# A hybrid RWKV/attention layer on one core: recurrence outputs moved to PSUM tiles of their own, two small copies to ScalarE, and the inverse stage called one wave later

## The chip, the core and the metric

The kernel runs on one core of a Trainium2 chip. The metric is device microseconds of one execution. The core's engines are TensorE (PE, with its weight load shown as PEld), VectorE (DVE), ScalarE (ACT), GpSimd (POOL) and the queue that issues most of the DMAs (SP). Each engine runs its own instructions in the order in which the program lists them, and waits on semaphores for the others.

## What is computed

Two layers of a backbone for 256 context tokens and 1024 latent tokens of width 1024. Each layer projects the stream, runs three kinds of heads (a bidirectional RWKV-7 recurrence, grouped-query attention, neighbourhood attention), gates them, projects back and normalises. What the change touches is the recurrence:

```python
def _rwkv7_step(S, inp):
    r, w, k, v, kk, b = inp
    sa = jnp.einsum('bhvk,bhk->bhv', S, kk)
    S = S * w[:, :, None, :] - sa[..., None] * b[:, :, None, :] + v[..., None] * k[:, :, None, :]
    return S, jnp.einsum('bhvk,bhk->bhv', S, r)
...
    S_f, y_f = lax.scan(_rwkv7_step, S0_f, (r, decay[:, :, 0], kd[:, :, 0], v, kk, bd[:, :, 0]))
    S_b, y_b = lax.scan(_rwkv7_step, S0_b, (r, decay[:, :, 1], kd[:, :, 1], v, kk, bd[:, :, 1]), reverse=True)
    return S_f, S_b, y_f + y_b
```

## The kernel before

The recurrence (`rwkv`, once per layer) is done in blocks. A **step** covers 32 tokens of both directions, a **wave** is four steps (128 tokens), and there are 10 waves per layer. Its parts, with the letters by which the last loop (L790 on) calls them:

- `wave_pre` (p) loads a wave's tensors and makes decays (`lp`, `iv`), the keys `kb`, the matrices `G` and the step decays `dc` (L575). `wave_gram` (g) multiplies `kb` with `G` and masks the result back into `G` (L616). `wave_kt` (k) transposes `kb` and copies it into `S` (L630).
- `wave_low` (l) writes triangular blocks to DRAM (`ls_d`) and reads them back in another layout (`lin`, L601). `wave_inv` (i) copies `lin` to `nn` (L635, L636), inverts in 15 rounds of two DVE operations (L644, L646) and sends the result through DRAM to `di`. `wave_merge` (m) makes `tt` from `di` with two groups of matmuls (`mg`, L675) and DVE operations L678 and L680.
- `wave_chain` is the serial part. Each step: 12 matmuls `rs` (L704), ACT copies them to `rsb` (L710), 12 matmuls `sa` (L715), four copies into the step's state `X` (L721), 12 matmuls `z` (L725), and two DVE operations that make the next step's `X` (L730). The output `y` of a step (`out_step`: 12 matmuls L742 and a copy to `yst`, L744) is put off through the list `pend` until the `rs` matmuls of the next step are written. In layer 1 the first two waves have no output.
- `out_block` adds both directions of `y` for one block of 128 tokens, normalises them, transposes them on PE (`pso`, L780; read by ACT at L782) and writes `yg_d`. Two blocks follow each of waves 6 to 9; in layer 0 two follow wave 1.

`X` has three buffers, so the loads of a step's `X` (four DMAs per step, L697, and four POOL memsets, L699) wait until the step three before is read to the end, by its `y` too. In PSUM the chain has one bank, `ch`: `rs`, `sa`, `z` and `y` are column ranges of it. All other stages take tiles in turn from the pool `pa`, which has **two** buffers (tag `pp`).

The projections that remain and the whole attention are written behind `rwkv`; a list scheduler sets each engine's order when the kernel is built, so the attention's instructions stand between those of the recurrence. Behind the recurrence stands what reuses its memory: the output weights (`wf<-wout`, L1110) and the output projection (L1159 on).

Of the kernel before, what the change touches and what calls it, by code (L numbers as in the profile page):

```python
# [8 lines left out]
F32 = mybir.dt.float32  # L9
# [34 lines left out]
def body(tc, a):  # L44
    nc = tc.nc
# [12 lines left out]
    pp = const.tile([128, DEPTH, NPC], F32, tag="pp", name="pp")  # L58
# [453 lines left out]
    def rwkv(l, lay):  # L512
# [3 lines left out]
        r2 = es.enter_context(tc.tile_pool(name=f"rx{l}", bufs=1, reuse_waits="tile"))  # L516
        r3 = es.enter_context(tc.tile_pool(name=f"ry{l}", bufs=1, reuse_waits="tile"))
        pb = es.enter_context(tc.tile_pool(name=f"pb{l}", bufs=1, space=PSUM))
        pa = es.enter_context(tc.tile_pool(name=f"pa{l}", bufs=2, space=PSUM))
        bank = pb.tile([128, 512], F32, tag="ch", name="ch")  # L520
        rs = sa = bank[:, 0:192].rearrange("p (c v) -> p c v", c=3)
        z = bank[:, 0:384].rearrange("p (d c v) -> p d c v", d=2, c=3)
        y = bank[:, 320:512].rearrange("p (c v) -> p c v", c=3)
        zw = lay["zw"]
        tri = rp.tile([128, 2, 128], F32, tag="tri", name="tri")
        nc.sync.dma_start(out=tri, in_=a["tri"])
# [6 lines left out]
        for g in S:  # L533
            for p in range(2):
                o = slice(64 * p, 64 * p + 64)
# [10 lines left out]
        def wave_pre(w):  # L546
            dc = r2.tile([128, 2, 4, 3], F32, tag="dc", name="dc", bufs=4)
            prep[w] = dict(dc=dc, d=[], g=[])
            for d in range(2):
                t0 = 128 * wave_block(w, d)  # L550
                need_r = not (last and t0 < TC)
                ld = {}
                for nm, ix in (("r", 0), ("kk", 1), ("kd", 2 + d), ("bd", 4 + d)):
                    if nm == "r" and not need_r:
                        continue
                    t = r3.tile([128, 3, 128], F32, tag="ld" + nm, name="ld" + nm, bufs=2 if nm == "r" else 1)
                    nc.sync.dma_start(out=t, in_=rw_d[ix, :, :, t0:t0 + 128].rearrange("c p t -> p c t"))
                    ld[nm] = t
                ps = pa.tile([128, 384], F32, tag="pp", name="psz")
                zs = r2.tile([98, 128], F32R, tag="zs", name="zs")  # L560
                nc.gpsimd.dma_start(out=zs, in_=zs_d[d, :, t0:t0 + 128])
                nc.tensor.matmul(out=ps, lhsT=zs, rhs=zw[d], start=True, stop=True)
                th = r3.tile([128, 384], F32, tag="th", name="th")
                nc.scalar.activation(out=th, in_=ps, func=AF.Tanh, scale=0.5)
                nc.vector.tensor_scalar(out=th, in0=th, scalar1=1.0, scalar2=None, op0=ALU.add)
                cu = pa.tile([128, 3, 4, 32], F32, tag="pp", name="pcu")
                for c in range(3):
                    nc.tensor.matmul(out=cu[:, c], lhsT=th[:, 128 * c:128 * c + 128], rhs=tri[:, d], start=True, stop=True)
                lp = r2.tile([128, 3, 4, 33], F32, tag="lp", name="lp")
                iv = r3.tile([128, 3, 4, 32], F32, tag="iv", name="iv")  # L570
                o = 1 - d
                nc.gpsimd.memset(lp[:, :, :, 32 * d:32 * d + 1], 1.0)
                nc.scalar.activation(out=lp[:, :, :, o:o + 32], in_=cu, func=AF.Exp, scale=-0.5 * EM05)
                nc.scalar.activation(out=iv, in_=cu, func=AF.Exp, scale=0.5 * EM05)
                nc.vector.tensor_copy(dc[:, d], lp[:, :, :, 32 * o:32 * o + 1].rearrange("p c j o -> p (j o) c"))  # L575
                kb = r2.tile([128, 3, 4, 64], F32, tag="kb", name="kb", bufs=2)
                v4 = lambda t: t.rearrange("p c (j t) -> p c j t", t=32)
                nc.vector.tensor_tensor(out=kb[:, :, :, 32 * d:32 * d + 32], in0=v4(ld["kd"]), in1=iv, op=ALU.mult)
                nc.gpsimd.tensor_tensor(out=kb[:, :, :, 32 - 32 * d:64 - 32 * d], in0=v4(ld["bd"]), in1=iv, op=ALU.mult)
                g = G[(2 * w + d) % 6]  # L580
                for p in range(2):
                    rs_ = slice(64 * p, 64 * p + 64)
                    gv = g[rs_, :, :, p, :].rearrange("q j c f -> q c j f")
                    nc.gpsimd.memset(g[64 - 64 * p:128 - 64 * p, :, :, p, 0:64 if need_r else 32], 0.0)
                    nc.gpsimd.tensor_tensor(out=gv[:, :, :, 0:32], in0=v4(ld["kk"])[rs_], in1=lp[rs_, :, :, d:d + 32], op=ALU.mult)
                    if need_r:
                        nc.gpsimd.tensor_tensor(out=gv[:, :, :, 32:64], in0=v4(ld["r"])[rs_], in1=lp[rs_, :, :, o:o + 32], op=ALU.mult)
                prep[w]["g"].append(g)
                prep[w]["d"].append((kb, 64 if need_r else 32))
# [93 lines left out]
        def wave_chain(w):  # L683
# [5 lines left out]
            for j in range(4):  # L689
# [10 lines left out]
                for c in range(3):  # L700
                    for d in range(2):
                        for p in range(2):
                            q = QSA[d][p]
                            nc.tensor.matmul(out=rs[q:q + 32, c, :], lhsT=gs[d][:, jc[d], c, p, 0:32], rhs=x[:, d, c, p, :],  # L704
                                             start=True, stop=True, tile_position=(0, q))
                for f in pend:
                    f()
                pend.clear()
                rsb = r2.tile([128, 3, 64], F32, tag="rsb", name="rsb")
                nc.scalar.copy(rsb, rs)  # L710
                for c in range(3):
                    for d in range(2):
                        for p in range(2):
# [21 lines left out]
            pend.clear()  # L735

        def out_step(w, j, x, jc, gs, yst):
            for c in range(3):
                for d in range(2):
                    for p in range(2):  # L740
                        q = QSA[d][p]
                        nc.tensor.matmul(out=y[q:q + 32, c, :], lhsT=gs[d][:, jc[d], c, p, 32:64], rhs=x[:, d, c, p, :],  # L742
                                         start=True, stop=True, tile_position=(0, q))
            nc.vector.tensor_copy(yst[:, j], y)  # L744
            if j == 3:
                for d in range(2):
                    for p in range(2):
                        q = QSA[d][p]
                        nc.sync.dma_start(out=y_d[d, 128 * w:128 * w + 128, :][:, 192 * p:192 * p + 192].rearrange("(j t) f -> t j f", t=32),
                                          in_=yst[q:q + 32].rearrange("t j c v -> t j (c v)"))  # L750
# [39 lines left out]
        for w in range(-3, NW):  # L790
            if w >= 0:
                wave_chain(w)
            for c in "kpglmi":
                v = w + (2 if c in "km" else 3)
                if 0 <= v < NW:
                    stages[c](v)
            for i, b in enumerate((11 - w, w) if w > 5 else (0, 1) if w == 1 and not last else ()):
                out_block(b, i)
# [593 lines left out]
```

## Time and profile before

| | us |
|---|---|
| runs of before | 2510.26 (median), 2495.68, 2519.41 |
| the profiled execution | 2503.84, its span 2502.0 |
| recurrence of layer 0, first `rs` to last `y` | about 402 to 1085 |
| recurrence of layer 1, the same | about 1673 to 2336 |
| busy share of PE, DVE, POOL, ACT | 88%, 66%, 47%, 39% |

The span is that of one profiled execution. A row of a view names an engine, a line of the kernel and the tile written and read; "idle before" is time that the engine stood still, and the arrow names what ended it. A matmul of 32-bit data is counted as two instructions, so 12 matmuls show as x24. PEclk is the granted share of TensorE's full clock.

### The profile page before, as it was taken

The numbers are of one execution on the slowest core, as the hardware profiler recorded it, in microseconds if no ns is written. First come the engines' busy times: TensorE is split into PE (matmuls) and PEld (weight loads), VectorE is DVE, ScalarE is ACT, GpSimd is POOL, SyncE is SP. The second block draws the span as 40 slices with busy tenths as digits, with TensorE's granted clock in tenths as the row PEclk, the third lists the DMA queues.
The fourth block names the chain that finished last, engine by engine and source line by source line (L and its number), as shares of the span: only waits on it lengthen the run. The fifth ranks groups of instructions, "written<-read, shape, count | busy, mean of one in ns | idle before, by whom it ended". The sixth has DMA issues, their size and how long they took to land.

```text
span 2502.0 us, 57786 instructions
## 1 busy us (share of the span) xinstructions
PE 2204.5 (88%) x22616; PEld 1655.1 (66%) x22616; DVE 1660.7 (66%) x3183; ACT 978.7 (39%) x2074; POOL 1188.3 (47%) x1438
## 2 busy tenths in 40 slices
PE   6989999986878798999899999999868788989897
PEld 4777898764555555555797777787655555645497
DVE  5686524546887778676386795524478787777746
ACT  3333413333544344554234434223334434445522
POOL 3464426335564454453246356334456545545443
PEclk9999999997898899989999999999869989989899
DMA  7345335446555434452332455335555444432332
GB/s 278 111 158 167 109 92 127 114 108 142 120 123 115 109 93 106 125 156 60 99 100 90 138 166 184 104 88 130 143 113 126 92 105 107 96 81 66 122 113 93
DMA packets 448241, 298.17 MB, mean 119 GB/s; under 512 B 249600, under 2 KB 395880, under 8 KB 446944
## 3 DMA queue, kind: packets, MB, share of 16 engines
q1 hardware_dynamic: 439936, 281.71, 41.2%
q0 software_dynamic: 7392, 10.28, 1.5%
q8 instruction: 178, 2.92, 0.5%
q10 hardware_dynamic: 640, 2.49, 0.4%
q14 instruction: 95, 0.78, 0.1%
HBM read 198.37 MB, written 91.79 MB: 116 GB/s over the span
## 4 chain that ended last, share of the span: by engine, by line
PE 47%; DVE 21%; DMA 14%; issue 6%; ACT 5%; SPq 4%; POOL 3%; DVEq 0%; POOLq 0%; ACTq 0%
PE pj L203 5%; PE pj L204 5%; PE pj L205 5%; PE y L921 4%; DMA ls_d<-G 3%; PE sm L867 2%; PE st L936 2%; DVE mx L869 2%; DVE e L646 2%; DMA lin<-ls_d 2%; PE pj L1159 2%; PE st L937 2%; DVE G L616 2%; PE pj L1161 2%; PE pj L1160 2%
## 5 line engine op out<-in xcount | busy, mean ns | idle before, releaser
L204 PE MATMUL pj<-hlo,wh 128*128 128x512 f32 (+1 forms) x1072 | 403.0, 376 | 12.3 <-DVE hlo L480 7.2
L203 PE MATMUL pj<-hhi,wh 128*128 128x512 f32 (+1 forms) x1072 | 404.9, 380 | 7.4 <-ACT qr L348 4.7
L205 PE MATMUL pj<-hhi,wl 128*128 128x512 f32 (+1 forms) x1072 | 400.8, 375 | 0.0
L204 PEld LDWEIGHTS pj<-hlo,wh 128*128 128x128 f32 x1072 | 205.6, 192 | 54.9 <-DVE hlo L480 7.3
L169 POOL TENSOR_TENSOR wl<-wf,wh 128x512 fp32r<-128x512 f32 x104 | 142.2, 1371 | 209.3 <-ACT wh L168 194.6
L203 PEld LDWEIGHTS pj<-hhi,wh 128*128 128x128 f32 x1072 | 205.0, 192 | 52.8 <-issue 7.0
L943 ACT ACTIVATE pt<-st 128x512 f32<-128x512 f32 (+1 forms) x292 | 165.2, 582 | 174.7 <-PE st L937 171.4
L205 PEld LDWEIGHTS pj<-hhi,wl 128*128 128x128 f32 x1072 | 205.5, 192 | 37.7 <-issue 3.1
L869 DVE TENSOR_REDUCE mx<-sm 128x1 f32<-128x512 f32 (+1 forms) x372 | 198.9, 553 | 39.2 <-PE sm L867 37.5
L921 PE MATMUL y<-pt,v 128*64 128x256 f32 (+1 forms) x1392 | 221.2, 406 | 2.7 <-ACT pt L943 2.3
L936 PE MATMUL st<-q,k 128*128 128x512 f32 (+3 forms) x376 | 168.0, 451 | 22.6 <-DVE am L110 6.5
L867 PE MATMUL sm<-k,q 128*128 128x256 f32 (+2 forms) x436 | 169.7, 432 | 19.5 <-DVE mx L869 7.8
L1159 PE MATMUL pj<-yh,wh 128*128 128x256 f32 x576 | 160.0, 294 | 11.8 <-ACT yh L1133 10.7
L1160 PE MATMUL pj<-yl,wh 128*128 128x256 f32 x576 | 164.7, 289 | 0.8 <-POOL yl L1134 0.8
L1161 PE MATMUL pj<-yh,wl 128*128 128x256 f32 x576 | 163.2, 288 | 0.0
L921 PEld LDWEIGHTS y<-pt,v 128*64 128x64 f32 x1392 | 97.1, 146 | 96.3 <-issue 66.3
L950 POOL TENSOR_TENSOR acc<-acc,pt 128x512 f32<-128x512 f32 x80 | 104.5, 1306 | 116.5 <-ACT pt L943 109.9
L937 PE MATMUL st<-q,k 65*128 65x512 f32 (+3 forms) x376 | 151.3, 406 | 1.4 <-ACT q L881 1.3
L867 PEld LDWEIGHTS sm<-k,q 128*128 128x128 f32 x436 | 84.8, 210 | 81.6 <-issue 21.0
L616 DVE TENSOR_TENSOR G<-gt,msk 64x192 f32<-64x192 f32 (+1 forms) x320 | 110.5, 345 | 39.6 <-PE gt L611 28.7
L699 POOL MEMSET X<- 32x192 f32 x320 | 82.9, 259 | 93.2 <-PE ch L742 68.8
L630 ACT COPY S<-kt 64x192 f32<-64x192 f32 x320 | 100.4, 314 | 55.4 <-PE ch L725 28.7
(276 smaller groups left out, 5137.2 us busy)
## 6 DMA issues: line engine op xcount, KB each, us to landing
wf<-win SPq DMA_DIRECT2D x104, 256.0 KB
wm<-wmod SPq DMA_DIRECT2D x32, 512.0 KB
yf<-yg_d SPq DMA_DIRECT2D x72, 128.0 KB
wt<-wm SPq DMA_DIRECT2D x8, 1024.0 KB
gate_d<-o SPq DMA_DIRECT2D x32, 256.0 KB
wf<-wout SPq DMA_DIRECT2D x16, 512.0 KB
ldkk<-rw_d SPq DMA_DIRECT2D x40, 192.0 KB
ldkd<-rw_d SPq DMA_DIRECT2D x40, 192.0 KB
```

Of the source, the lines that this page charges most:

```text
L203: nc.tensor.matmul(out=ps[:, :n], lhsT=wh, rhs=hhi[:, k, t0:t0 + n], start=(k == 0), stop=False)
L204: nc.tensor.matmul(out=ps[:, :n], lhsT=wh, rhs=hlo[:, k, t0:t0 + n], start=False, stop=False)
L205: nc.tensor.matmul(out=ps[:, :n], lhsT=wl, rhs=hhi[:, k, t0:t0 + n], start=False, stop=(k == KT - 1))
L867: nc.tensor.matmul(out=sp_[:, :o], lhsT=q[0][:, qc:qc + 128], rhs=k[0][:, c0:c0 + o], start=True, stop=True)
L869: nc.vector.tensor_reduce(out=mx[:, n_:n_ + 1], in_=sp_[:, :o], op=ALU.max, axis=AX.X)
L921: mm = nc.tensor.matmul(out=y[64 * i:64 * i + 64, a0:a1], lhsT=v[:, t, :], rhs=pt[:, p0:p0 + a1 - a0], start=start, stop=stop and at == le ...
L936: nc.tensor.matmul(out=o, lhsT=k[0][:, 128 * t:128 * t + 128], rhs=q[0][:, qa:qb], start=True, stop=False)
L937: mm = nc.tensor.matmul(out=o, lhsT=k[1][0:65, 128 * t:128 * t + 128], rhs=q[1][0:65, qa:qb], start=False, stop=True)
L943: nc.scalar.activation(out=pt[:, :w], in_=sp_[:, :w], func=AF.Exp)
L1159: nc.tensor.matmul(out=p_, lhsT=wh[m][:, k], rhs=yh, start=(x_ == 0), stop=False)
L1160: nc.tensor.matmul(out=p_, lhsT=wh[m][:, k], rhs=yl, start=False, stop=False)
L1161: nc.tensor.matmul(out=p_, lhsT=wl[m][:, k], rhs=yh, start=False, stop=(x_ == KT - 1))
```

## The change

Three edits. The recurrence output gets a tile `py` of the pool `pa` instead of columns of `ch`, its copy to `yst` goes from DVE to ACT, and the put-off outputs are written behind the copy of `rs` instead of ahead of it. The copy of the step decays `dc` goes from DVE to ACT. The stages of a loop pass are called in another order: `i` comes first, for wave w + 2, where it came last, for wave w + 3.

```diff
-        y = bank[:, 320:512].rearrange("p (c v) -> p c v", c=3)
...
-                nc.vector.tensor_copy(dc[:, d], lp[:, :, :, 32 * o:32 * o + 1].rearrange("p c j o -> p (j o) c"))
+                nc.scalar.copy(dc[:, d], lp[:, :, :, 32 * o:32 * o + 1].rearrange("p c j o -> p (j o) c"))
...
+                rsb = r2.tile([128, 3, 64], F32, tag="rsb", name="rsb")
+                nc.scalar.copy(rsb, rs)
                 for f in pend:
                     f()
                 pend.clear()
-                rsb = r2.tile([128, 3, 64], F32, tag="rsb", name="rsb")
-                nc.scalar.copy(rsb, rs)
...
         def out_step(w, j, x, jc, gs, yst):
+            y = pa.tile([128, 3, 64], F32, tag="pp", name="py")
...
-            nc.vector.tensor_copy(yst[:, j], y)
+            nc.scalar.copy(yst[:, j], y)
...
-            for c in "kpglmi":
-                v = w + (2 if c in "km" else 3)
+            for c in "ikpglm":
+                v = w + (2 if c in "ikm" else 3)
```

First place: PE in the last wave of layer 1, from the middle of the wave to its last step. `X_17548` (after: `X_17588`) is the state buffer of the wave's first and last step, `X_17549` and `X_17550` (after: `X_17589`, `X_17590`) those of the two between. Before:

```order
L704 MATMUL ch<-X_17550,G_17530 32x64 x2
L704 MATMUL ch<-X_17550,G_17531 32x64 x2
...
L742 MATMUL ch<-X_17549,G_17530 32x64 x2
L742 MATMUL ch<-X_17549,G_17531 32x64 x2
...
L715 MATMUL ch<-rsb,tt 32x64 x12
...
L725 MATMUL ch<-X_17550,S_17538 64x64 x6
...
L704 MATMUL ch<-X_17548,G_17530 32x64 x2
```

After:

```order
L780 MATMUL pso<-c_ident,yo 128x128 x3
L742 MATMUL py<-X_17588,G_17570 32x64 x2
...
L867 MATMUL sm<-k_25912,q_26520 128x512
L867 MATMUL sm<-k_25912,q_26520 128x256
L921 MATMUL y<-pt_26767,v 64x256
...
L969 MATMUL ls<-acc_26529,onec 32x256 x2
...
L742 MATMUL py<-X_17589,G_17570 32x64 x2
...
L703 MATMUL ch<-X_17588,G_17570 32x64 x2
L742 MATMUL py<-X_17590,G_17570 32x64 x2
```

Before, each step's `y` stood directly behind the next step's `rs`. After, the `y` of the wave's first three steps stand together behind the second `pso` of the blocks that follow the wave before, and the last step's `rs` stands among them; where no block follows a wave, they stand behind the second `mg` group of the wave after.

Second place: DVE in layer 1, from the masks of the last wave (`G<-gt,msk`) to its inverse (`nn<-lin`, then `tmp<-nn,e`). Before:

```order
L616 TENSOR_TENSOR G_17531<-gt,msk 64x3x64 x4
L950 TENSOR_TENSOR acc_25860<-acc_25860,pt_25956 128x512
L770 TENSOR_SCALAR sm<-sm 128x6
L869 TENSOR_REDUCE mx<-sm 128x1
L771 TENSOR_TENSOR yo<-yo,sm 128x384
...
L636 COPY nn<-lin 64x256
L869 TENSOR_REDUCE mx<-sm 128x1
L644 TENSOR_TENSOR tmp<-nn,e 128x15
```

After:

```order
L615 TENSOR_TENSOR G_17571<-gt,msk 64x3x64 x4
L869 TENSOR_REDUCE mx<-sm 128x1 x2
L950 TENSOR_TENSOR acc_25599<-acc_25599,pt_25866 128x512
L776 TENSOR_TENSOR yo<-yo,sm 128x2x3x64
...
L635 COPY nn<-lin 64x256
L869 TENSOR_REDUCE mx<-sm 128x1
L643 TENSOR_TENSOR tmp<-nn,e 128x15
```

Between the last masks and the second `nn` stand eleven rows before and six after, and the same kinds of rows; in none of the 20 waves does the `nn` of a wave move behind another wave's masks.

## Rows read from the trace of the kernel before

**Rows 1.** The page's first part: busy us (share of the span) and instructions.

```profile
PE 2204.5 (88%) x22616; PEld 1655.1 (66%) x22616; DVE 1660.7 (66%) x3183; ACT 978.7 (39%) x2074; POOL 1188.3 (47%) x1438
```

**Rows 2.** Busy time by stretch: both recurrences, and layer 1's passage to the output.

```profile
core 0: us, PE busy (x) PEld busy (x) DVE busy (x) ACT busy (x) POOL busy (x), PEclk, DMA share, GB/s
400.00:1100.00 700.00, 594.09 (x8668) 414.07 (x8668) 490.03 (x1266) 299.50 (x722) 332.14 (x448) 0.90 0.49 119
...
1700.00:2345.00 645.00, 552.97 (x7992) 371.36 (x7990) 474.86 (x1183) 282.01 (x656) 325.39 (x434) 0.90 0.44 105
2340.00:2380.00 40.00, 29.51 (x143) 16.45 (x142) 31.84 (x38) 21.29 (x37) 19.62 (x12) 0.77 0.48 154
```

**Rows 3.** Timelines of PE, DVE, ACT, one step: start, length, instruction [idle before].

```profile
2216.82 0.54 PE L704 MATMUL ch<-X,G 128*32 128x64 f32 x24
2217.18 0.52 PE L742 MATMUL ch<-X,G 128*32 128x64 f32 x24
...
2219.49 0.35 DVE L744 COPY yst<-ch 128x192 f32<-128x192 f32 x1
...
2219.93 0.32 ACT L710 COPY rsb<-ch 128x192 f32<-128x192 f32 x1 [3.65 <-DVE yst L744]
```

**Rows 4.** Waits, whole span: total us, times, longest.

```profile
ACT rsb L710 <- DVE yst L744: 94.3, 33, 12.2
...
DVE nn L636 <- DMA lin<-ls_d: 73.4, 17, 8.1
...
PE kt L626 <- DVE tt L680: 25.4, 11, 5.1
...
PE ch L715 <- ACT rsb L710: 18.4, 10, 5.3
```

**Rows 5.** Groups by line: busy us, mean ns | idle before, and releasers.

```profile
L575 DVE COPY dc<-lp 128x12 f32<-128x12 f32 x40 | 28.5, 711 | 56.8 <-ACT lp L573 56.6
...
L744 DVE COPY yst<-ch 128x192 f32<-128x192 f32 x72 | 25.3, 351 | 16.9 <-PE ch L742 15.7 <-DMA stg<-q_d 0.5
...
L710 ACT COPY rsb<-ch 128x192 f32<-128x192 f32 x80 | 25.5, 319 | 106.8 <-DVE yst L744 94.3 <-PE ch L704 5.8 <-DVE G L616 2.3
```

**Rows 6.** Line L626 (`kt`, PE and PEld): idle before it, us, times.

```profile
  DVE tt L680: 55.0, 22
  ACT S L630: 7.0, 12
```

**Rows 7.** DMA issues: ns min/median/max on SP; a POOL-issued load, us to landing.

```profile
L697 SPq DMA_DIRECT2D X<-vt_d x320: 537/570/1888, 372.3 to 2303.8; - x160
...
zs<-zs_d POOLq DMA_DIRECT2D x40, 49.0 KB, 2.3
```

**Rows 8.** PE timeline: attention work behind the last step's `rs`, layer 1.

```profile
2326.67 0.54 PE L704 MATMUL ch<-X,G 128*32 128x64 f32 x24
...
2327.48 0.94 PE L867 MATMUL sm<-k,q 128*128 128x256 f32 x2
2328.34 1.08 PE L921 MATMUL y<-pt,v 128*64 128x256 f32 x8
2329.36 0.63 PE L969 MATMUL ls<-acc,onec 128*32 128x256 f32 x4
...
2332.12 0.55 PE L780 MATMUL pso<-c_ident,yo 128*128 128x128 f32 x3
```

**Rows 9.** PE timeline: a last step's `rs`, and second `pso` of blocks ahead.

```profile
1077.96 0.54 PE L704 MATMUL ch<-X,G 128*32 128x64 f32 x24
...
1100.66 0.90 PE L780 MATMUL pso<-c_ident,yo 128*128 128x128 f32 x3
...
2232.66 0.52 PE L780 MATMUL pso<-c_ident,yo 128*128 128x128 f32 x3 [1.81 <-issue]
```

**Rows 10.** Timelines of PE and DVE: a last step's `rs`, and a later `tt`.

```profile
2143.45 0.54 PE L704 MATMUL ch<-X,G 128*32 128x64 f32 x24 [0.86 <-DVE X L730]
...
2153.40 0.55 DVE L680 TENSOR_TENSOR tt<-mg,di 128x384 f32<-128x384 f32 x1
```

## The prediction, made before the changed kernel ran

> **What bounds the kernel now.** I read the page's busy line first: PE is busy for 88% of the span, no other engine for more than 66% [rows 1]. So time is lost where PE stands idle or runs at a lower clock. The table by stretch shows where: in the two recurrences PE is busy for 594.09 of 700 us and for 552.97 of 645 us [rows 2], so it stands idle for 106 and 92 us, 198 us together, and its granted clock is 0.90 there. In these stretches attention fills the gaps between the steps of the recurrence. A change to the recurrence is worth what it takes out of these 198 us, and not what it takes off the recurrence alone.
>
> Next I read one step in the timeline [rows 3]. `rs` runs at 2216.82 and lasts 0.54 us, `y` of the step before follows at 2217.18. The copy of that `y` waits in DVE's queue behind other work until 2219.49. Only when it is done does ACT copy `rs` (2219.93, after 3.65 us of idleness that the `y` copy ended) and `sa` can follow. So the `y` copy sits in the serial chain, though nothing in the chain reads it. The list of waits gives its size over the span: ACT waited for the `y` copy 33 times, 94.3 us in all [rows 4]. Yet PE, which has attention rows between `rs` and `sa`, waited for `rsb` in only 10 places, 18.4 us [rows 4].
>
> **The change part by part.** The sum is made against the profiled execution, 2503.84 us, which lies 6.4 us under the median of the runs of before (2510.26). The same steps can be applied to either.
>
> *Chain freed of the `y` copy.* The 94.3 us of ACT waiting go. PE can gain at most the 18.4 us that it waited there, and at least nothing, since the new order puts fewer attention rows between `rs` and `sa`, too. I take half: **−9 us**.
>
> *Less work on DVE.* The 72 `y` copies (25.3 us) and the 40 `dc` copies (28.5 us) leave it [rows 5]: 53.8 of 1660.7 us [rows 1], 3.2%. The 56.6 us that DVE waited for `lp` ahead of `dc` [rows 5] do not go: the next instruction in its queue, `kb` (L578), reads `iv`, which ACT makes right after `lp`. If every idle microsecond of PE in the two stretches scaled with DVE's load, 3.2% of 198 us would be 6 us. Bounds: 0, and 54 us if all of it lay on the path. I take **−5 us**.
>
> *More work on ACT.* 72 copies at the 319 ns of the same shape (L710) are 23 us, and 40 `dc` copies at no more than that are 13 us. ACT is busy 39% of the time and loses 94.3 us of blocked time. Bounds 0 and 36 us; I take **+1 us**.
>
> *The inverse one wave later.* DVE waited 73.4 us for `lin` at L636 [rows 4]. The edit is to give that transfer a wave's time. The order shows that it does not: the scheduler still places `nn` a few rows behind the masks of its own wave, in all 20 waves. The transfer therefore still lands late: **0 us**. Were the 73.4 us to go, the same scaling (4.4% of 198 us) would give −9 us.
>
> *Outputs in the pool `pa`.* Here the change adds waits. The pool has two buffers, and they are handed out in the order of the program text. So the first output of a wave now stands behind the merge of the next wave, or, where blocks follow, behind their `pso` tiles; and `kt` stands behind the last outputs. Before, `kt` was the tile behind the merge, and PE waited 25.4 us for `tt` there [rows 4]. Now mostly `y` stands there, so that wait moves and does not grow: 0. What is added is 28 `kt` tiles and 36 `y` tiles that wait for the ACT copy of a `y` tile. The nearest row is `kt` behind ACT's copies: 7.0 us [rows 6] over 80 `kt` tiles, 0.09 us each, but these have more rows between them than many of the new pairs (in nine cases `kt` follows with hardly a row between). I take twice that, 0.18 us, for 64 tiles: **+11 us**; bounds 0 and, with the whole copy of 0.319 us exposed each time, 20 us.
>
> *The last step of a wave waits for its first output.* `X` has three buffers, so step 3 of a wave loads into the buffer that the `y` of step 0 reads. Before, that `y` was long done. In the new order it stands just ahead of the `rs` of step 3. Between the two lie four DMA issues on SP of 0.57 us each and a landing; the trace gives no landing for this load, and the nearest row is a load of 49 KB in 2.3 us [rows 7]. My estimate is 4 × 0.57 + 2.3 = 4.6 us. PE has, in the place that the order shows, about 3.9 us of rows there: attention rows like those of [rows 8] (0.7 for two `sm`, 1.08 for `y`, 1.2 for two `ls`, 0.4 for one `st`) and 0.5 for the second `y`. 0.7 us are left open per wave, in 18 waves with outputs, and not in all of them: **+9 us**. Bounds 0 and 18 × 4.6 = 83 us. SP's queue stands at that load as well, and the loads queued behind it (`wf`, `stg`) start later; POOL's queue at its memset. I cost that at nothing, as attention has these tiles in two buffers.
>
> *Layer 0 ends its recurrence later.* Its second block lies far behind the last step now (`rs` at 1077.96, `pso` at 1100.66 [rows 9]), so the chain is held there and the scheduler has put attention rows into the gap. The attention that was left behind the recurrence covers the hold; about a third of it is still left there in the new order. What may be uncovered is the load of the output weights, which wait for the recurrence's memory. Layer 1 shows that price already: 10.5 us of PE idleness in 2340 to 2380 [rows 2]. I take **+2 us**, bounds 0 and 10.5.
>
> **Sum**: −9 −5 +1 +0 +11 +9 +2 = +9 us, 2513 us against the profiled execution; on the median of the runs, **2519 us**. I forecast no change that can be told: about 1% is what a measurement of this kernel can tell from none, as the three runs of before span 0.95%.
>
> On the pool the Trainium skill (Perfetto Trace Analysis, Optimization Strategy) speaks against this change: the same gap repeating on the engine that should be saturated can mean that there is not enough PSUM for the next tile. The trace agrees as far as it goes: behind `tt` the `kt` line shows such a gap 22 times [rows 6]. By that rule the 72 new tiles would each meet it at the `kt` line's mean, (55.0 + 7.0) / 80 = 0.78 us, 56 us instead of 11, and the sum would be 2564 us.
>
> **The rivals.**
>
> *Faster: the chain sets layer 1.* Layer 1 has no attention left behind its recurrence, so if its PE idleness is owed to the chain, the freed wait comes back in full there. Of 72 `y` copies 32 are layer 1's: 94.3 × 32/72 = 42 us, and DVE's −5. With the added waits hidden, that is 2510 − 47 = **2463 us**; with half of the added waits, about 2475. For it speaks the 3.65 us of [rows 3]. Against it: PE waited for `rsb` only 18.4 us in the whole span, and the new order places the last wave's steps of layer 1 no earlier among the attention rows. It needs the merges and the `pso` tiles to be done before step 3 is due.
>
> *Slower: the chain is held by the pool in layer 1.* The second `pso` of the blocks behind wave 6 ran at 2232.66, the `rs` of step 3 of the next wave had run at 2216.82 [rows 3, 9]: 16 us earlier, and it may no longer. In the last wave the two were at 2332.12 and 2326.67 [rows 8], 5 us. Where no block follows, the merge decides: a `tt` ended at 2153.95, and the step 3 that now has to come after it had its `rs` at 2143.45 [rows 10], 10 us. That is 31 us, and the reload's 4.6 us in four waves are 18 more. Layer 1 has nothing to cover them. Less the gains of 14 us it gives +35: **2545 us** on the median. It decides as soon as a `pso` or `tt` ends after the step 3 that now waits for it would be due; if the blocks, which now stand ahead of an inverse in the program text, come sooner, it falls away.
>
> *The inverse does move on the chip*, since its transfer has landed for other reasons: −9 us, 2510 us. It changes no verdict.
>
> **How the numbers follow.** The forecast (within 1%, 2485 to 2535) gets 0.47: its gains and losses are small and of both signs. Faster by over 1% gets 0.24, as PE's own waits leave it little room. Slower by over 1% gets 0.29, as the added waits stand in every wave. The range runs from 2478, near the faster rival with half of the added waits, to 2556, past the slower rival; it leaves out about 2 in 10, most of it below. The forecast's own range is 2490 to 2535.
>
> **What the changed profile would show.** Right: no row of ACT waiting for `yst`; `rsb` waiting for `rs` alone; PE's wait for `tt` at L742 in place of `kt`, some 25 us; DVE's wait for `lin` still at 70 to 90 us; DVE at about 1610 us busy; PE idle within 15 us of 198 in the two recurrences. Wrong: a `lin` wait under 30 us would say that the inverse did move. PE idle in layer 1 down by 30 us would say that the chain sets it. A PE wait at the `rs` line for `X` loads, or at L742 for `pso`, of over 40 us would say that the pool holds the chain.

## The result, and the profile after

The changed kernel takes 2486.22 us (15 runs, 2472.85 to 2496.35) where the kernel before, on the same chip, takes 2505.39: a ratio of 0.9938, 95% interval 0.9918 to 0.9957. It is 0.62% faster, about 16 us, within 1% as forecast, but on the other side: 2519 had been predicted. (The ratio is not the quotient of the two medians; that is 0.9923, or 19 us, and lies within the interval.) The profiled span fell from 2502.0 to 2485.9 us.

The page's first part of the changed kernel, beside [rows 1]:

```profile
PE 2207.0 (89%) x22616; PEld 1648.8 (66%) x22616; DVE 1644.2 (66%) x3071; ACT 1004.3 (40%) x2186; POOL 1183.7 (48%) x1438
```

53.8 us of copies left DVE, and its busy time fell by 16.5, since other instructions of DVE took longer: 112 `acc` additions (L950) took 114.7 us where they had taken 97.6, and 300 `tmp` products (L643, before L644) 89.7 where they had taken 77.5. ACT took up 25.6.

Next, busy time by stretch. [rows 2] cut at round numbers; here each recurrence goes from its first `rs` to its last `z`. First the changed kernel, then the kernel before with its own bounds:

```profile
core 0: us, PE busy (x) PEld busy (x) DVE busy (x) ACT busy (x) POOL busy (x), PEclk, DMA share, GB/s
402.60:1152.40 749.80, 649.50 (x8953) 438.40 (x8956) 512.75 (x1263) 334.13 (x824) 350.38 (x461) 0.91 0.46 112
1670.70:2317.30 646.60, 570.22 (x8095) 386.39 (x8097) 473.31 (x1175) 299.97 (x724) 332.46 (x442) 0.93 0.46 107
```

```profile
402.30:1084.30 682.00, 578.16 (x8580) 405.19 (x8582) 477.49 (x1240) 292.86 (x711) 323.75 (x439) 0.91 0.49 117
1673.40:2335.60 662.20, 571.13 (x8089) 387.96 (x8091) 484.51 (x1224) 288.98 (x675) 332.13 (x442) 0.90 0.44 104
```

Layer 0's recurrence grew by 68 us, and layer 1 still starts 2.7 us sooner: attention that used to follow has been done inside it. Layer 1's recurrence shrank by 15.6 us, nearly the whole gain of this profiled pair (what follows it takes 168.6 us, before 166.4). PE's idle time there fell from 662.20 − 571.13 = 91 us to 76 us, and its granted clock rose from 0.90 to 0.93.

The waits of the changed kernel that answer to [rows 4]:

```profile
ACT rsb L706 <- PE ch L703: 66.5, 28, 9.2
DVE kb L577 <- ACT iv L573: 54.6, 19, 9.3
DVE nn L635 <- DMA lin<-ls_d: 50.5, 17, 8.3
...
DVE nn L634 <- DMA lin<-ls_d: 22.0, 9, 10.0
...
PE py L742 <- DVE tt L679: 14.3, 4, 8.8
...
PE ch L714 <- ACT rsb L706: 10.8, 8, 3.9
...
PE kt L625 <- DVE tt L679: 4.3, 3, 2.5
```

`rsb` no longer waits for the `y` copy (94.3 us before) but mostly for `rs`, 66.5 of its 86 us. PE's wait for `rsb` fell from 18.4 to 10.8 us. The wait for `tt` went from `kt` (25.4) to `y` and `kt` together (18.6). DVE's wait for `lin` fell from 86.2 us over both lines to 72.5. The groups by line that answer to [rows 5]:

```profile
L577 DVE TENSOR_TENSOR kb<-ldkd,iv 128x384 f32<-128x384 f32 x40 | 45.4, 1136 | 65.0 <-ACT iv L573 54.6 <-DMA ldkd<-rw_d 3.9 <-POOL wl L169 3.7
...
L744 ACT COPY yst<-py 128x192 f32<-128x192 f32 x72 | 22.5, 318 | 46.1 <-PE py L742 45.1 <-DMA gtl<-gate_d 0.4
L574 ACT COPY dc<-lp 128x12 f32<-128x12 f32 x40 | 8.6, 216 | 0.2
```

Here is the first thing that I had passed over. The same 40 `dc` copies that took 28.5 us on DVE (711 ns each) take 8.6 us on ACT (216 ns). The `y` copies cost nearly the same on both (351 and 318 ns).

### The profile page after: what moved, and what is told of

Read it like the earlier page. It is cut to its first block, busy times and chain, and to the rows that moved or that the text cites. A ratio compares the mean times of both kernels' runs of the same rounds, so it can differ in the third digit from the quotient of the medians.

```text
span 2485.9 us, 57805 instructions
## 1 busy us (share of the span) xinstructions
PE 2207.0 (89%) x22616; PEld 1648.8 (66%) x22616; DVE 1644.2 (66%) x3071; ACT 1004.3 (40%) x2186; POOL 1183.7 (48%) x1438
## 4 chain that ended last, share of the span: by engine, by line
PE 43%; DVE 22%; DMA 15%; issue 7%; ACT 5%; POOL 4%; SPq 4%; DVEq 0%; POOLq 0%; ACTq 0%
PE pj L204 5%; PE pj L203 5%; PE pj L205 5%; PE y L921 3%; DMA yf<-yg_d 2%; PE sm L867 2%; DVE G L615 2%; DMA ls_d<-G 2%; PE st L936 2%; DVE tmp L643 2%; DVE mx L869 2%; PE st L937 2%; DVE e L645 2%; PE ch L724 1%; DMA lin<-ls_d 1%
## 5 line engine op out<-in xcount | busy, mean ns | idle before, releaser
L869 DVE TENSOR_REDUCE mx<-sm 128x1 f32<-128x512 f32 (+1 forms) x372 | 198.9, 553 | 56.6 <-PE sm L867 54.9
L921 PEld LDWEIGHTS y<-pt,v 128*64 128x64 f32 x1392 | 96.6, 146 | 93.0 <-issue 64.5
L950 POOL TENSOR_TENSOR acc<-acc,pt 128x512 f32<-128x512 f32 x80 | 105.9, 1324 | 95.1 <-ACT pt L943 94.7
L950 DVE TENSOR_TENSOR acc<-acc,pt 128x512 f32<-128x512 f32 x112 | 114.7, 1034 | 16.9 <-ACT pt L943 14.9
```

Source lines behind the costliest of these rows:

```text
L869: nc.vector.tensor_reduce(out=mx[:, n_:n_ + 1], in_=sp_[:, :o], op=ALU.max, axis=AX.X)
L921: mm = nc.tensor.matmul(out=y[64 * i:64 * i + 64, a0:a1], lhsT=v[:, t, :], rhs=pt[:, p0:p0 + a1 - a0], start=start, stop=stop and at == le ...
L950: eng.tensor_tensor(out=acc[i][:, :w], in0=sums[i][:, :w], in1=pt[:, :w], op=ALU.add)
```

## The experiments

Every kernel ran five rounds beside the kernel before, on the same chip, so the ratios have intervals of 0.2% to 0.4% to either side. The theories that stand in the expectations: A, the pool holds the chain, and the copies gain; B, the edits share one gain; C, what the scheduler happens to make of a kernel decides; D, the gain is DVE's time, which splits into D1 (its load wherever it stands) and D2 (its place ahead of `kb`). Theories 1 to 3, and E, are explained where they stand. Waves are counted through both layers: 0 to 9 are layer 0's, 10 to 19 layer 1's.

### Each edit alone

Its own tile for `y`, and its place behind the `rsb` copy (the copy stays on VectorE):

```
-        y = bank[:, 320:512].rearrange("p (c v) -> p c v", c=3)
...
+                rsb = r2.tile([128, 3, 64], F32, tag="rsb", name="rsb")
+                nc.scalar.copy(rsb, rs)
                 for f in pend:
                     f()
                 pend.clear()
-                rsb = r2.tile([128, 3, 64], F32, tag="rsb", name="rsb")
-                nc.scalar.copy(rsb, rs)
...
+            y = pa.tile([128, 3, 64], F32, tag="pp", name="py")
```

> Only the first edit's PSUM part: y in tiles of the pool and written behind the copy of rs; its copy to yst stays on DVE, dc on DVE, the stages in the old order. Theory 1 (the gain of the whole change, 0.6%, is the chain freed of the y copy): 0.4 to 0.8% faster than before, ACT's wait for yst at L710 gone. Theory 2 (the gain is work taken off DVE): no gain, 0 to 1% slower, because the pool's waits are added and nothing is taken off DVE. Theory 3 (the gain is the stage order): 0 or slower.

2527.13 us, ratio 1.0066 [1.0041, 1.0091]: slower by 17 us. The other three edits are one line each of the change:

```
-            nc.vector.tensor_copy(yst[:, j], y)
+            nc.scalar.copy(yst[:, j], y)
```

> Only the copy of y to yst goes from DVE to ACT; y stays in the chain's bank, ahead of the copy of rs. The copy of rs still comes after the y copy, but both are now neighbours in ACT's own queue, so DVE's queue is out of the chain. Theory 1: 0.4 to 0.8% faster, like the whole change or better, because the pool's waits are not added. Theory 2: 0.2 to 0.4% faster (25 us of DVE's 1661 us). Theory 3: same.

2502.83 us, 0.9978 [0.9956, 0.9999].

```
-                nc.vector.tensor_copy(dc[:, d], lp[:, :, :, 32 * o:32 * o + 1].rearrange("p c j o -> p (j o) c"))
+                nc.scalar.copy(dc[:, d], lp[:, :, :, 32 * o:32 * o + 1].rearrange("p c j o -> p (j o) c"))
```

> Only the copy of the step decays goes from DVE to ACT. Theory 1: same within 0.2%. Theory 2: 0.2 to 0.5% faster (28 us off DVE). Theory 3: same.

2485.34 us, 0.9922 [0.9892, 0.9952]: this one line gives 20 us, as much as the whole change or more, and more than theory 2 allowed.

```
-            for c in "kpglmi":
-                v = w + (2 if c in "km" else 3)
+            for c in "ikpglm":
+                v = w + (2 if c in "ikm" else 3)
```

> Only the order in which the stages of a pass are called (the inverse first, one wave later). Theory 1 and 2: same within 0.3%, DVE's wait for lin at 70 to 90 us as before. Theory 3: 0.4 to 0.8% faster, lin's wait below 50 us, or the blocks that follow a wave done earlier against the next wave's steps.

2512.76 us, 1.0013 [0.9992, 1.0034]: no effect that can be told.

### The change without one edit

> The changed kernel without its PSUM edit: y stands in the chain's bank again and its copy ahead of the rsb copy, on ScalarE; the decay copies on ScalarE and the stage order are kept. Theory A (the pool holds the chain: the tile edit alone cost 0.66%, and the decay copies alone gave 0.78%): faster than the change, 2470 to 2485 us, ratio 0.984 to 0.990; in layer 1 the wave 17 step 2 to step 3 takes 23 us as in the kernel before, not 38. Theory B (the edits share one gain, the chain's own time in layer 1, and no more than some 16 us is to be had there): as the change, ratio 0.990 to 0.996. Theory C (what a schedule happens to be decides, and single edits do not add): anywhere within 0.99 to 1.01.

2486.34 us, 0.9895 [0.9862, 0.9929]. The ratio is theory A's, though its interval reaches into B's range, and the median lies 1 us above A's. In the trace wave 17's step 2 to step 3 takes 14 us.

> The changed kernel with the y copies left on VectorE (25 us of work there). Theory A (the pool holds the chain; copies that wait longer in VectorE's queue hold the pool longer, too): ratio 0.997 to 1.003, about 0.3% to 0.8% above the change. Theory B (the decay copies carry the gain and the rest sums to nothing): as the change, 0.991 to 0.996.

2501.52 us, 0.9971 [0.9948, 0.9993]: theory A's range, not B's.

> The changed kernel with the decay copies left on VectorE. Theory A and B (the decay copies carry the gain): the gain is gone, ratio 0.998 to 1.008, and by the sum of the single edits (0.66% - 0.22% + 0.13%) 1.006. Theory C (a schedule's luck): anywhere, below 0.996 as well.

2501.77 us, 0.9970 [0.9941, 1.0000]: just below the range of A and B, and well below the 1.006 of the sum.

> The changed kernel with the stages in the old order, the inverse behind the blocks. The order edit alone gave 1.0013 [0.9992, 1.0034]. Theory A and B: as the change, ratio 0.991 to 0.997. If the inverse's place matters once the copies are off VectorE (its wait for lin was 86 us before and 72 after), the time rises by up to 14 us to a ratio of 0.999.

2495.65 us, 0.9937 [0.9915, 0.9960].

The order does nothing (0.9937 without it, 0.9938 with it). The tile costs 17 us alone and some 11 as the last edit. As the last edit, each of the two copy edits is worth about 8 us, half of the gain: 0.9970 and 0.9971 against 0.9938. So `dc`, 20 us alone, is worth less beside the tile, and `y`, 5.5 us alone, no less; but these differences of 8 and 11 us are no larger than two intervals together. Alone, the four sum to −0.21%; together they give −0.62%. From the tile alone (1.0066) to the change the other three edits bring 1.28%, by themselves 0.87%. The runs don't settle how the edits combine.

### Does the pool hold the chain?

The changed kernel with the blocks of a wave written behind the next wave's chain:

```
             if w >= 0:
                 wave_chain(w)
+            for b, i in late:
+                out_block(b, i)
             for c in "ikpglm":
...
-            for i, b in enumerate((11 - w, w) if w > 5 else (0, 1) if w == 1 and not last else ()):
-                out_block(b, i)
+            late = [(b, i) for i, b in enumerate((11 - w, w) if w > 5 else (0, 1) if w == 1 and not last else ())]
+        for b, i in late:
+            out_block(b, i)
```

> The changed kernel with each wave's output blocks written into the program one wave later, behind the next wave's chain: the pso tiles then stand behind that wave's outputs in the pool, nothing else changes. Theory A (the pool holds the chain: in the changed kernel step 2 to step 3 of wave 17 takes 38.5 us, of wave 19 23 us): the two take 23 and 13 to 18 us, layer 1's recurrence is 10 to 25 us shorter than 646.6, the ratio 0.984 to 0.990. Theory B (nothing more to be had once the copies are moved): 0.990 to 0.996; the blocks end later, and layer 1's tail grows by what the recurrence gains.

2477.71 us, 0.9901 [0.9867, 0.9934], against 0.9938 for the change. The PE timeline of the changed kernel, layer 1, wave 17 (start, length, instruction):

```profile
2161.53 0.43 PE L703 MATMUL ch<-X,G 128*32 128x64 f32 x16
...
2171.30 0.52 PE L780 MATMUL pso<-c_ident,yo 128*128 128x128 f32 x3
...
2196.06 0.49 PE L780 MATMUL pso<-c_ident,yo 128*128 128x128 f32 x3
2196.47 0.54 PE L742 MATMUL py<-X,G 128*32 128x64 f32 x24
2199.64 0.54 PE L742 MATMUL py<-X,G 128*32 128x64 f32 x24
2200.01 0.25 PE L703 MATMUL ch<-X,G 128*32 128x64 f32 x2
```

The `rs` of step 2 ran at 2161.53, that of step 3 at 2200.01, 38 us later; before, the two were at 2194.19 and 2216.82, 23 us. The first output of the wave runs directly behind the second `pso` of the blocks ahead, and step 3 directly behind the outputs. With the blocks one wave later the same place reads:

```profile
2171.16 0.54 PE L703 MATMUL ch<-X,G 128*32 128x64 f32 x24
...
2182.08 0.54 PE L742 MATMUL py<-X,G 128*32 128x64 f32 x24
2189.46 0.87 PE L742 MATMUL py<-X,G 128*32 128x64 f32 x24 [4.99 <-DVE tt L679]
...
2196.53 0.87 PE L703 MATMUL ch<-X,G 128*32 128x64 f32 x24
```

25 us. What is left is the merge's `tt`, 4.99 us of PE idleness. In wave 19 the step takes 12.1 us (23.0 in the change). Layer 0 has the longest holds: there step 2 to step 3 takes 70.1 us in wave 2 and 57.2 in wave 7 of the changed kernel, 15.2 and 21.6 before, and 19.5 and 18.3 with the late blocks. Attention filled most of these holds: PE's idle time in layer 0's recurrence was 103.8 us before, 100.3 in the changed kernel and 88.0 with the late blocks. So the hold is there and its place is the one that the edit moved. In time the gain is 0.37%, some 9 us, no more than the two intervals together allow for chance, and 0.9901 lies on the border of the ranges of A and B. Layer 1's recurrence is only 3 us shorter, and what follows it is 11 us longer, as theory B had said; the rest was gained ahead of layer 1.

### Why the decay copies cost so much on VectorE

These tests put the copy elsewhere. First, `dc` on ScalarE with VectorE's load put back beside it, in a copy that nobody reads:

```
                 nc.scalar.copy(dc[:, d], lp[:, :, :, 32 * o:32 * o + 1].rearrange("p c j o -> p (j o) c"))
+                dq = r2.tile([128, 12], F32, tag="dq", name="dq")
+                nc.vector.tensor_copy(dq.rearrange("p (j c) -> p j c", c=3), lp[:, :, :, 32 * o:32 * o + 1].rearrange("p c j o -> p (j o) c"))
```

> The decay copies alone on ScalarE (ratio 0.9922 by itself), and beside each a VectorE copy of the same shape from the same lp into a tile that nobody reads: VectorE's 28 us of work and its wait for lp are back, the use of dc stays with ScalarE. Theory D (the gain is VectorE's time: 28.5 us of stretched copies in a queue that sets the recurrence): 0.998 to 1.003. Theory E (the gain is that dc comes sooner, or that the schedule moved): stays at 0.989 to 0.996.

2515.26 us, 1.0036 [1.0011, 1.0062]: the gain is gone, theory E falls. Then on GpSimd:

```
-                nc.vector.tensor_copy(dc[:, d], lp[:, :, :, 32 * o:32 * o + 1].rearrange("p c j o -> p (j o) c"))
+                nc.gpsimd.tensor_copy(dc[:, d], lp[:, :, :, 32 * o:32 * o + 1].rearrange("p c j o -> p (j o) c"))
```

> The kernel before with the decay copies on GpSimd in place of VectorE: off VectorE too, but on an engine that is 47% busy and that shares the wave's preparation. Theory D: 0.990 to 0.996, as on ScalarE. Theory C: anywhere in 0.99 to 1.01. If GpSimd's queue, which makes kb, gates and the X zeros, sets a part of the wave: 1.000 to 1.006.

2472.31 us, 0.9877 [0.9841, 0.9912]: the gain is there, and beyond the range of theory D, so it is owed to leaving VectorE and not to ScalarE. It need not be the same gain all through: in the one profile of each, PE's idle time is 15.9 us less than before with `dc` on ScalarE and its busy time 2.7 us less; on GpSimd it is 9.1 us of idle and 28.5 us of busy time, at a mean granted clock of 0.934 where the kernel before had 0.926. Two more moved the VectorE copy behind `kb` in the program text, once as `dc` itself (the diff) and once as the unread copy `dq`:

```
-                nc.vector.tensor_copy(dc[:, d], lp[:, :, :, 32 * o:32 * o + 1].rearrange("p c j o -> p (j o) c"))
...
                 nc.vector.tensor_tensor(out=kb[:, :, :, 32 * d:32 * d + 32], in0=v4(ld["kd"]), in1=iv, op=ALU.mult)
+                nc.vector.tensor_copy(dc[:, d], lp[:, :, :, 32 * o:32 * o + 1].rearrange("p c j o -> p (j o) c"))
```

> The kernel before with the decay copy still on VectorE, but written behind kb in place of ahead of it: VectorE's 28.5 us of work stay, kb no longer queues behind the copy. Theory D1 (VectorE's load wherever it stands): 0.998 to 1.003. Theory D2 (what counts is the copy ahead of kb, whose start it delays by some 20 us in 40 places): 0.989 to 0.996, as with the copy on ScalarE. Theory C (the schedule's luck): anywhere.

2504.67 us, 1.0005 [0.9980, 1.0030].

> The decay copies on ScalarE, and VectorE's copy of the same shape from lp into a tile that nobody reads now stands behind kb in the program text (ahead of it in the run before, which gave 1.0036). Theory D1 (load): 0.998 to 1.004 again. Theory D2 (the place ahead of kb): 0.989 to 0.996.

2511.68 us, 1.0023 [1.0007, 1.0039].

Neither tells load from place: the scheduler put the copy ahead of `kb` all the same, since `lp` is ready before `iv`. The row of the first shows it, `kb` waiting for almost nothing behind a copy that waits for `lp`:

```profile
L577 DVE TENSOR_TENSOR kb<-ldkd,iv 128x384 f32<-128x384 f32 x40 | 40.2, 1006 | 5.7 <-ACT iv L574 3.2 <-DMA ldkd<-rw_d 2.3
L578 DVE COPY dc<-lp 128x12 f32<-128x12 f32 x40 | 31.0, 774 | 56.4 <-ACT lp L573 56.3
```

So the last one reads `kb`, and must stand behind it:

```
-                nc.vector.tensor_copy(dq.rearrange("p (j c) -> p j c", c=3), lp[:, :, :, 32 * o:32 * o + 1].rearrange("p c j o -> p (j o) c"))
+                nc.vector.tensor_copy(dq.rearrange("p (j c) -> p j c", c=3), kb[:, :, :, 32 * d:32 * d + 1].rearrange("p c j o -> p (j o) c"))
```

> The decay copies on ScalarE, and VectorE copies as many elements from kb, right behind the instruction that makes kb, into a tile that nobody reads: the load is back in VectorE's queue, but behind kb (in the two runs before, where it read lp, the scheduler put it ahead of kb both times: 1.0036 and 1.0023). Theory D1 (load wherever it stands): 0.998 to 1.004. Theory D2 (the place ahead of kb): 0.989 to 0.996.

2491.05 us, 0.9927 [0.9907, 0.9948]. VectorE carries the load and the gain stays. Its rows, and those of the first test:

```profile
L578 DVE TENSOR_TENSOR kb<-ldkd,iv 128x384 f32<-128x384 f32 x40 | 42.4, 1060 | 64.1 <-ACT iv L574 49.7 <-DMA ldkd<-rw_d 8.7 <-POOL wl L169 3.3
...
L580 DVE COPY dq<-kb 128x12 f32<-128x12 f32 x40 | 22.7, 566 | 0.5
```

```profile
L580 DVE TENSOR_TENSOR kb<-ldkd,iv 128x384 f32<-128x384 f32 x40 | 41.2, 1030 | 4.8 <-ACT iv L574 3.5 <-DMA ldkd<-rw_d 0.9 <-DMA gate_d<-o 0.2
L577 DVE COPY dq<-lp 128x12 f32<-128x12 f32 x40 | 29.6, 741 | 66.5 <-ACT lp L573 66.3
```

22.7 us of copies behind `kb` cost nothing that can be told; 29.6 us ahead of it cost the whole gain. The two copies differ in what they read as well, `kb` or `lp`; but the waits that the trace puts down to the `lp` copy of the first test are under 2 us in all. In these kernels what counts is how long VectorE waits and copies before it gets to `kb`. The rows for the kernel before and for `dc` on ScalarE (the row of `dc` before stands in [rows 5]):

```profile
L578 DVE TENSOR_TENSOR kb<-ldkd,iv 128x384 f32<-128x384 f32 x40 | 41.5, 1037 | 5.6 <-ACT iv L574 2.8 <-DMA ldkd<-rw_d 2.3 <-DMA gate_d<-o 0.2
```

```profile
L578 DVE TENSOR_TENSOR kb<-ldkd,iv 128x384 f32<-128x384 f32 x40 | 45.4, 1135 | 69.4 <-ACT iv L574 58.7 <-DMA ldkd<-rw_d 4.5 <-POOL wl L169 3.7
```

Added up from such rows (idle before the copy, the copy, idle before `kb`), for the kernels without the tile edit:

| kernel | VectorE ahead of `kb`, us | ratio |
|---|---|---|
| dc + unread copy from lp | 100.9 | 1.0036 |
| the same, written behind kb | 98.2 | 1.0023 |
| order alone | 96.6 | 1.0013 |
| two stages exchanged | 96.2 | 1.0008 |
| dc written behind kb | 93.1 | 1.0005 |
| before | 90.9 | 1 |
| y copies on ScalarE | 84.1 | 0.9978 |
| y and dc off VectorE, new order (dc on GpSimd) | 71.9 | 0.9801 |
| dc on ScalarE | 69.4 | 0.9922 |
| the same with dc on ScalarE | 67.1 | 0.9895 |
| dc on GpSimd | 66.8 | 0.9877 |
| dc on ScalarE, unread copy from kb | 64.1 | 0.9927 |

From 90.9 to 69.4 is 21.5 us, and 0.78% of 2510 is 19.6 us. Between these two the microseconds come out of the span nearly one for one; among the kernels at 64 to 72 us the order is no longer kept, and the six kernels at 90.9 us and more differ by little more than their intervals. Each value is one profile's (that of the `y` copies on ScalarE is of the slowest of their 12 runs, 2515.29 us), and no single wait of PE shows the gain: with `dc` on ScalarE its idle time falls from 297.5 to 281.6 us over the span in small pieces. By which of PE's waits `kb` sets the pace is left open.

The kernels with the tile edit do not keep this rate. The change without the `dc` edit has these rows:

```profile
L577 DVE TENSOR_TENSOR kb<-ldkd,iv 128x384 f32<-128x384 f32 x40 | 38.7, 968 | 6.1 <-ACT iv L573 3.2 <-DMA ldkd<-rw_d 2.4
L574 DVE COPY dc<-lp 128x12 f32<-128x12 f32 x40 | 22.4, 560 | 62.3 <-ACT lp L572 62.2
```

That is 90.8 us at a ratio of 0.9970; the change has 65.0 at 0.9938. 25.8 us fewer ahead of `kb` come out as some 8 us of time, and the two intervals overlap. The change without the `y` edit stands at 0.9971 with 64.5, the tile alone at 1.0066 with 89.0. So the place ahead of `kb` accounts for the `dc` edit by itself; what takes most of its worth in the tile's company, the runs do not show.

Why the copy is slow, the trace of the kernel before shows. DVE's timeline at one `dc` copy of layer 1, and POOL's:

```profile
2167.76 2.15 DVE L575 COPY dc<-lp 128x12 f32<-128x12 f32 x1 [0.74 <-ACT lp L573]
2169.82 0.55 DVE L578 TENSOR_TENSOR kb<-ldkd,iv 128x384 f32<-128x384 f32 x1
```

```profile
2166.84 1.26 POOL L950 TENSOR_TENSOR acc<-acc,pt 128x512 f32<-128x512 f32 x1
2168.07 0.92 POOL L585 TENSOR_TENSOR G<-ldkk,lp 64x384 f32<-64x384 f32 x1
2168.95 0.92 POOL L587 TENSOR_TENSOR G<-ldr,lp 64x384 f32<-64x384 f32 x1
2169.95 1.21 POOL L585 TENSOR_TENSOR G<-ldkk,lp 64x384 f32<-64x384 f32 x1
```

The copy of 12 elements per partition runs 2.15 us and ends at 2169.91, as POOL's third instruction ends (2169.87) and before its next one starts; `kb` follows. 15 of the 40 copies take over 0.5 us, 23.0 of the 28.5 us together, and every one of the 15 ends 0.03 or 0.04 us after a POOL instruction does. Two of the three POOL instructions here read the `lp` that released the copy, so the meeting is built in. The three copies with no POOL work beside them took 0.17 us on average, and so did five that began 0.05 to 0.10 us ahead of a POOL instruction that makes `G`.

The Trainium skill (SBUF — State Buffer, Who interferes with whom) states this: VectorE and GpSimd share a pair of ports under an exclusive lock, plain copies are among the instructions that may take it, and whoever comes second "fully blocks". The trace agrees, with 15 endings of 15. ScalarE has ports of its own by that page; its 40 copies took 203 to 237 ns. It would have been the rule to weigh, and the 711 ns of [rows 5] were the hint.

### A schedule moved with nothing else changed

```
-            for c in "kpglmi":
+            for c in "kpgmli":
```

> The kernel before with the stages l (low transfers of wave w+3) and m (merge of wave w+2) exchanged in the program text, which touch nothing in common: no instruction is added, removed or changed. Theory D: 0.998 to 1.002. Theory C (a reshuffled schedule alone moves the time by as much as the edits do): outside 0.995 to 1.005.

2508.97 us, 1.0008 [0.9983, 1.0033]. With the order edit and the copy behind `kb`, three reshuffles moved the time by 0.05% to 0.13%. Three are few, but they speak against theory C as an account of 0.8%. An earlier try at such a reshuffle exchanged other stages than its text says:

> The kernel before with two neighbouring stages in the program text exchanged (the merge ahead of the inverse of another wave): no instruction is added, removed or changed, only the order into which the scheduler puts them moves. Theory C (what a schedule happens to be decides): may land anywhere within 0.990 to 1.010, outside its own interval of 1. Theories A and B: 0.998 to 1.002, as the stage order alone gave 1.0013.

It swapped g and l, so that the low transfers left before the gram products had written what they carry: a part of the computation is changed, and its 2550.44 us (1.0182) say nothing here.

### Versions that combine

The late blocks and the change, with `dc` on GpSimd:

> The changed kernel with the output blocks one wave later (ratio 0.9901 by itself) and the decay copies on GpSimd in place of ScalarE (alone 0.9877 against 0.9922 on ScalarE). If the two add: 0.984 to 0.988, 2465 to 2475 us, ahead of both kernels. If the gain is one and the same (some 16 to 25 us that layer 1's recurrence can give): 0.987 to 0.991.

2480.65 us, 0.9912 [0.9882, 0.9941]: no more than the late blocks alone, so here GpSimd in place of ScalarE adds nothing. And without the tile: both copies off VectorE (`y` to ScalarE, `dc` to GpSimd), the new order, `y` back in the chain's bank:

> No tile of its own for the outputs, y copies on ScalarE, stage order of the change (0.9895 with the decay copies on ScalarE), and the decay copies on GpSimd (alone 0.9877). If the gains add over that of ScalarE: 0.984 to 0.988, 2465 to 2475 us. If it is one and the same gain, as the late blocks with GpSimd gave 0.9912 against 0.9901: 0.988 to 0.992.

2460.34 us, 0.9801 [0.9775, 0.9828]: 50 us under the kernel before and some 34 under the change. It beats both, by more than the parts promised: it differs from the change without the tile (0.9895) in nothing but the engine of `dc`, and VectorE has more ahead of `kb` in it, 71.9 us against 67.1. So the account by VectorE's queue doesn't explain this step of 0.9%. Its first part of the page:

```profile
PE 2174.6 (88%) x22616; PEld 1640.7 (67%) x22616; DVE 1630.2 (66%) x3071; ACT 997.1 (41%) x2146; POOL 1191.1 (48%) x1478
```

PE is busy 30 us less than before for the same 22616 matmuls, at a mean granted clock of 0.935 over the span (before 0.926), and idle 285.4 us (before 297.5). Its five runs had mean clocks of 0.929 to 0.935, those of the kernel before beside them 0.917 to 0.931. With `dc` alone on GpSimd PE is busy 2176.0 us at 0.934. Why the clock is higher there was not tested.

## Why the prediction was wrong

*What bounds the kernel* held: the change's gain is in PE's idle time and its clock in layer 1's recurrence. That about 1% is the least that can be told from none did not: the interval is 0.2% to either side.

*Chain freed of the `y` copy, −9 us.* The wait went as described, and PE's wait for `rsb` fell by 7.6 us. What that is worth in time no run shows by itself: the change with late blocks, where the chain is freed and the hold is mostly gone, stands at 0.9901, and the change without the tile, where `y` still sits in the chain, at 0.9895. The pool's other waits are still in the first, so the two bound the term only loosely, at 0 within some 12 us.

*Outputs in the pool, +11, the reload, +9, layer 0, +2.* With the −9 these edits were to cost 13 us. Measured: 17 us alone, 11 us as the last edit (0.9938 against 0.9895). The sum came near, in part by luck: how it divides was not measured, the reload's price lies elsewhere than I put it, and layer 0's recurrence, for which I had 2 us, grew by 68, mostly covered by attention. PE's idleness ahead of the changed kernel's `rs` line (PE and its weight loads):

```profile
  DVE X L729: 28.0, 22
  POOL X L698: 18.0, 20
...
  DMA X<-vt_d: 1.6, 2
```

It is POOL's memset of `X`, which I had costed at nothing (18.0 us; in the kernel before it is not among the ten largest there), and not the load (1.6 us). DVE's `X`, the largest, was 18.4 us before. By the rule of the Trainium skill that I weighed (Perfetto Trace Analysis, Optimization Strategy) the tiles alone would have cost 56 us; all these edits together measured 17.

*The inverse, 0.* Right: order alone 1.0013, and 72.5 us of the `lin` wait stayed.

*Less work on DVE, −5, more on ACT, +1.* **This is the step that failed.** The two were to bring 4 us together. The change without the tile, which holds these copies and the order (no effect alone), is 1.05% faster: 26 us. The `dc` copies alone gave 20 us, the `y` copies 5.5. The tile takes 11 of the 26 again, which leaves the 15 us measured, but that is no check: the 11 us are the difference between these two kernels. Each edit alone would sum to 5 us. Even as the last edit beside the tile, either copy edit gave some 8 us. I had scaled PE's idleness by DVE's load, as if every microsecond of a queue weighed the same. I had rightly seen that the 56.6 us of waiting ahead of `dc` would move to `kb`; I had not asked what stands behind the copy in DVE's queue, nor why 12 elements per partition take 711 ns. What the runs showed in its place: unread copies of 29.6 us ahead of `kb` cost the whole gain of `dc`, 22.7 us behind it nothing that can be told. How far this holds beside the tile stays open.

*The rivals.* The faster one had the place right (layer 1); its reason is not borne out: the edit that frees the chain made the kernel slower by itself, pool waits included, and the `y` copy on ScalarE, which takes DVE's queue out of the chain without them, gave 5.5 us. The slower one had a true mechanism: in wave 17 step 3 comes 16 us later behind step 2 than before, in wave 19 10 us. But layer 1 came to these places sooner (wave 17's first `rs` at 2133.0, before at 2164.8, 32 us), and of that 13 us were given back in wave 17. Of what the profile was to show, two signs came out as written (no wait for `yst`, the `lin` wait at 72.5) and one nearly (`rsb` waiting for `rs`, 66.5 of 86 us). The wait for `tt` at the `y` line is 14.3 us, not some 25, DVE is busy 1644 us and not 1610, and PE's idleness in the recurrences fell by 18 us, more than 15.

## What to carry to other kernels

A microsecond taken off an engine is worth what stands behind it in that engine's queue: small copies cost 20 us or more ahead of `kb`, and nothing that could be told behind it. Such a price is that of one kernel: beside the tile edit the same move was worth 8 us, so measure an edit in the company in which it will run. Where a small instruction's mean is several times its shortest duration, look at what ends when its long ones end before sizing its move. When several pieces draw on one pool, try writing them into the program in the order in which they will be ready: it shortened the holds here (the longest from 70 us to 19), though attention had covered most of them and the time fell by no more than chance allows.

## What the hardware showed

A VectorE copy between SBUF tiles can last through several GpSimd instructions in a row. At 693.68 in the kernel before one took 4.88 us:

```profile
693.68 4.88 DVE L575 COPY dc<-lp 128x12 f32<-128x12 f32 x1
```

```profile
694.73 2.87 POOL L838 TENSOR_TENSOR k<-stg,k 64x1280 fp32r<-64x1280 f32 x1
697.55 0.11 POOL L572 MEMSET lp<- 128x12 f32 x1
697.61 0.92 POOL L587 TENSOR_TENSOR G<-ldr,lp 64x384 f32<-64x384 f32 x1
```

It ended at 698.56, 0.03 us after the last of these, and four POOL instructions that had begun after it ran meanwhile (the first at 694.32). The 72 `y` copies, which read PSUM, took 306 to 359 ns each and show nothing of it. The `dc` copy takes 0.16 to 4.88 us on VectorE in the kernel before, 0.20 to 0.24 us on ScalarE in the changed kernel and 0.19 to 0.65 us on GpSimd in the kernel with that move alone.
